# One hymba decoder block: the order of the gate tiles, the evacuation of the v rows, the PSUM banks of two helpers and five lead times of the planner

## The chip, the core and the metric

The kernel runs on one core of one Trainium2 chip. The metric is the device time of one execution in microseconds (us). TensorE (PE) does the matrix products into PSUM, VectorE (DVE) and ScalarE (ACT) read PSUM and work in SBUF, GpSimd (POOL) works in SBUF alone, and SyncE (SP) issues nearly all DMAs. Each engine takes its instructions strictly in its own order and waits on semaphores of the others.

## What is computed

One decoder layer for 1024 tokens and a model width of 1024. Two branches take their inputs from one projection of the normed input; the gates d and z (`z_d`, `z_s`), the three convolved inputs q, k, v and the state-space input u are each 512 wide.

```python
a = rms_norm(h, norm_mix_g)
proj = a @ w_in
u_s, z_s, q, k, v, z_d, b_raw, a_raw = jnp.split(proj, [...], axis=-1)
y_s = s5_branch(u_s, ...) * silu(z_s)          # diagonal state space, gelu, glu
# DeltaNet: q, k, v = silu(causal_conv(q, k, v)); q, k l2-normalised
# beta = sigmoid(b_raw); g = -exp(A_log) * softplus(a_raw + dt_bias)
# chunked gated delta rule over 128 rows, rms_norm, * silu(z_d)
mix = concat([y_s, y_d]) @ w_out
h = h + mix
h = h + sigmoid(h @ w_gate) * rms_norm(p @ w_ple_proj)
return rms_norm(h, final_norm_g)
```

## The kernel before

**Matrix products.** A weight tile of 128 columns is split into a high and a low part (`wh` by ScalarE, `wl` by VectorE), and every product is three matmuls over each of 8 slices of the contraction (`mm3`). An input tile (`inproj`, L615 to 630) makes two halves of 512 tokens; a half is 24 matmuls of 512 columns into one bank, here called for instance q0.0 and q0.1. ScalarE evacuates each half: two activations for q, k and v (`raw` and `cv`), one Silu for the gates d and z (`z`), one copy for u (`ut`). VectorE then does three shifted multiply-adds per convolved tile (`cv<-raw`, L700, recorded under the helper L103).

**PSUM.** The eight banks are in pools: `mm` has two and is taken by turns by `MM` and `MMs` (all halves, the sums of squares `ssp` of q and k, the b tail `pab`, and, before, the v transposes `vtp` and the products k k' `gps`). `MX` has three (the prefix products `pT`). `MS` is one, `MZ` two (S5's `hp`, `kps`, `inj`, `yps`, later the chunks).

**The order.** TensorE's order is written out by a planner (L1326 ff.). It keeps a clock that advances with an estimate of TensorE's work (`pec`), a list of chains, and a list of fillers. A chain yields either a name that must be done or a lead time from the table `LAT` (L474); until its clock time has come, fillers are placed. Other engines' instructions are placed by the framework by readiness. The chains are:

- `a_chain`: 64 steps n for the softplus input a. A step is three matmuls with the triangle (`tg`) and four with the diagonal (`dg`) into `pT`; ScalarE, one VectorE subtraction, ScalarE again, and four VectorE scans (L756) work it off. Steps are planned 5.2 us apart. Then `g_math` (L767) does softplus with small VectorE operations and gives `gg`; TensorE transposes it (`gtp`), a row stage, five transposes (`pe`), `decay`, `subst` (31 steps of a substitution on VectorE), `blocks`, `double` (`q32`, `d32`, `q64`, `d64`) and the eight chunks follow, each chunk in steps A, B and C into the banks `bk`.
- `s5_chain`: S5's parameters on VectorE, then four batches (`hp`, `kps`, a DMA round trip, `inj`, scans, `yps`).
- `attn_chain`: q k' (`kq`) after the loads of q.

Fillers stand in the string `FILL`: input tiles, S5's inputs u, the b columns, k k', GLU (`pg`), the output projections (`po`), the gate (`pq`). A tile of q, k or v may only start when the tail of the tile two before is done. The tails are the sums `ssp` (30.3 us of the clock after the tile), for v the four transposes per half (23.2 us), and for b the product `pab` with `sel` (11.4 us).

Of the kernel before, what the change touches and what calls it, by code (L numbers as in the profile page):

```python
# [16 lines left out]
P = 128  # L17
# [8 lines left out]
def hymba_block_kernel(ctx: ExitStack, tc: tile.TileContext, A: dict, out: bass.AP, dbg=None):  # L26
# [67 lines left out]
    def tt(e, o, a, b, op):  # L94
        return e.tensor_tensor(out=o, in0=a, in1=b, op=op)  # L95
# [277 lines left out]
    def s5_params():  # L373
# [98 lines left out]
    kpv = kp.rearrange("h (b j q) t -> b q j h t", j=4, q=2)  # L472

    LAT = dict(  # L474
        prep=20.0, ev=3.3, kps=5.0, scan=22.0, tab=6.0, g1=23.0, g2=4.0, dec=14.8, sub=25.0, blk=0.3,
        q32=6.9, d32=8.0, q64=2.0, d64=0.8, kq=4.3, A=1.4, B=4.8, C=1.4, otp=10.3, vtp=23.2, ssq=30.3,
        bs8=11.4, gl=15.1, par=13.8, xp=1.2, sse=1.5, ql=14.0,
    )
    s5t = {}

# [286 lines left out]
    def g_math():  # L767
        se = FT[0][:, 0:128].rearrange("p (a b c) -> p a b c", a=4, b=8)
        tt(V, se, se2[:, :, :, :, 0], se2[:, :, :, :, 1], SUB)
        tt(V, se[:, 0], se[:, 0], se[:, 1], ADD)  # L770
        tt(V, se[:, 2], se[:, 2], se[:, 3], ADD)
        tt(V, se[:, 0], se[:, 0], se[:, 2], ADD)
        tt(V, se[:, 0], se[:, 0], hb4[:, 4:8].unsqueeze(1).to_broadcast(SH), ADD)
        ax = flat(se[:, 0])


        gsc = FT[1][:, 0:1024]
        n36 = [0]
# [31 lines left out]
        for c in (0.4985410273075104, 6.578732490539551, 29.91191864013672, 60.949668884277344, 57.11296463012695):  # L810
            stt(V, lp, lp, c, ee, ADD, MUL)
        ts(V, lp, lp, 20.039552688598633, ADD)
        V.tensor_copy(out=lq, in_=ee)
        for c in (15.062909126281738, 83.04756927490234, 221.7624053955078, 309.0987243652344, 216.42788696289062):
            stt(V, lq, lq, c, ee, ADD, MUL)
        ts(V, lq, lq, 60.11865997314453, ADD)
        V.reciprocal(out=lq, in_=lq)
        tt(V, lp, lp, lq, MUL)
        tt(V, l2, ee, ee, MUL)
        tt(V, lq, ee, l2, MUL)  # L820
        tt(V, lp, lq, lp, MUL)
        stt(V, lp, l2, -0.5, lp, MUL, ADD)
        tt(V, lp, ee, lp, ADD)
        ts(V, lx, ee, 1.0, ADD, 0.5, MUL)
        ts(V, lx, lx, -1.0, ADD)
        tt(V, l2, lx, lx, MUL)
        tt(V, lx3, l2, lx, MUL)
        ts(V, la, lx, 0.07037683576345444, MUL)
        stt(V, la, la, -0.11514610052108765, lx, ADD, MUL)
        stt(V, la, la, 0.11676998436450958, lx3, ADD, MUL)  # L830
        ts(V, lb, lx, -0.12420140951871872, MUL)
        stt(V, lb, lb, 0.14249323308467865, lx, ADD, MUL)
        stt(V, lb, lb, -0.16668057441711426, la, ADD, ADD)
        tt(V, lb, lb, lx3, MUL)
        ts(V, lc, lx, 0.2000071406364441, MUL)
        stt(V, lc, lc, -0.24999994039535522, lx, ADD, MUL)
        stt(V, lc, lc, 0.3333333134651184, lb, ADD, ADD)
        tt(V, lc, lc, lx3, MUL)
        ts(V, lc, lc, -0.00021219444170128554, ADD)
        stt(V, l2, l2, -0.5, lx, MUL, ADD)  # L840
        tt(V, lc, l2, lc, ADD)
        ts(V, lc, lc, 0.693359375, ADD)
        ts(V, la, ee, 0.4142135679721832, ALU.is_lt)
        ts(V, lb, la, -1.0, MUL, 1.0, ADD)
        tt(V, lp, lp, la, MUL)
        tt(V, lc, lc, lb, MUL)
# [12 lines left out]
        tr(p[0:32, 0:P], flat(gg_), ident)
        V.tensor_copy(out=gt, in_=p[0:32, 0:P])  # L860
# [12 lines left out]
        ts(V, c2r[:, lo_], gc[:, lo_], gla, SUB)
        V.tensor_copy(out=c2r[:, up_], in_=gc[:, up_])
        V.tensor_copy(out=egr[:, lo_], in_=gc[:, lo_])
        ts(V, egr[:, up_], gc[:, up_], gla, ADD)
        ts(V, err_[:, lo_], c2r[:, lo_], -1.0, MUL, glb, ADD)
        ts(V, err_[:, up_], gc[:, up_], -1.0, MUL, glb, ADD)
        gls = C("gls", [32, 1])
        tt(V, gls, gla, glb, ADD)  # L880
        V.tensor_copy(out=egl_, in_=gls.to_broadcast([32, P]))
        yield LAT["g2"]
        pe5 = MX("pe5", [P, 5, 32])
        for x, r in enumerate((egr, err_, egl_, gc, c2r)):
# [68 lines left out]
    def gram(n):  # L953
        c, i = n // 2, n % 2
        if i == 0:
            zt[c] = T(f"zt{c}", F32, [P, 2, 4, P])
        p = MMs("gps", [P, 4, P])
        for h in range(4):
            mm(p[:, h, :], ksl(kk_, n, h), ksl(kk_, n, h))
        tt(V, zt[c][:, i], p, dd[:, 4 * n:4 * n + 4].unsqueeze(2).to_broadcast([P, 4, P]), MUL)  # L960
        yield 0
        done.add(f"g{n}")

    def v_tile(h):
# [594 lines left out]
```

## Time and profile before

| what | value |
|---|---|
| median of 3 runs | 910.13 us (903.36 to 910.64) |
| the profiled execution, its own time | 910.48 us |
| its span from first to last instruction | 908.7 us |
| PE busy | 795.3 us, 88% |
| DVE busy | 696.9 us, 77% |
| ACT busy | 491.6 us, 54% |
| POOL busy | 256.6 us, 28% |
| mean granted clock of PE | 0.927 |

A busy PE counts the modelled length of its matmuls, at whatever clock was granted; the column PEclk of the stage view tells the clock. The idle time in a row of instructions is that of its engine just before it, and the arrow names who ended it.

### The profile page before, as it was taken

Reading aid. Unit: us, or ns where it says so; the run is one execution under the profiler, and the core shown is the slowest. Engines: PE = TensorE matmul, PEld = TensorE weight load, DVE = VectorE, ACT = ScalarE, POOL = GpSimd, SP = SyncE. Lnnn points to the kernel's source line nnn. Section 1 sums busy time; section 2 is a strip of 40 time slices with the busy share of each in tenths; the row PEclk is TensorE's granted clock in tenths of the full one; section 3 lists DMA queues with packets and bytes.
Section 4 is the critical chain, followed back from the end, with each engine's and each line's share of the span. In section 5 each row is a group of like instructions: output and inputs, shape, how many; then the busy total and the mean of one; then the engine's idle time right before and its main releaser. Section 6 shows DMA issues by size and latency. Waiting matters only on the chain. (4 is left out here: it accounts for less than half of the span.)

```text
span 908.7 us, 12241 instructions
## 1 busy us (share of the span) xinstructions
PE 795.3 (88%) x4338; PEld 647.1 (71%) x4338; DVE 696.9 (77%) x1464; ACT 491.6 (54%) x922; POOL 256.6 (28%) x245
## 2 busy tenths in 40 slices
PE   4689977978995989799798996979899979899996
PEld 3578666856884867688677775868688858678885
DVE  5967968887886599869567989794977695528886
ACT  6678475686676777684768335144432243013343
POOL 0011844541424134503000011035432185302222
PEclk9799979986996997899999998979999998899998
DMA  9331103222031123032300243137562053202211
GB/s 334 128 115 30 64 11 89 83 57 67 9 93 46 53 70 90 27 117 98 90 4 24 70 138 118 67 99 184 151 220 96 33 162 128 70 1 93 75 41 70
DMA packets 67581, 79.93 MB, mean 88 GB/s; under 512 B 23456, under 2 KB 49344, under 8 KB 67520
## 3 DMA queue, kind: packets, MB, share of 16 engines
q1 hardware_dynamic: 67376, 78.89, 27.2%
q8 instruction: 34, 0.56, 0.3%
q10 hardware_dynamic: 144, 0.26, 0.1%
q14 instruction: 27, 0.22, 0.1%
HBM read 57.39 MB, written 21.74 MB: 87 GB/s over the span
## 5 line engine op out<-in xcount | busy, mean ns | idle before, releaser
L115 PE MATMUL pj<-ah,wh 128*128 128x512 f32 x384 | 158.6, 413 | 5.1 <-DVE ssq L914 4.1
L115 PE MATMUL pj<-al,wh 128*128 128x512 f32 x384 | 155.2, 404 | 0.0
L115 PE MATMUL pj<-ah,wl 128*128 128x512 f32 x384 | 155.1, 404 | 0.0
L106 ACT ACTIVATE F<-F,gridc 128x512 f32<-128x512 f32 x128 | 114.9, 987 | 0.0
L756 DVE TENSOR_TENSOR_SCAN F<-F,vst 128x192 f32<-128x192 f32 x128 | 86.9, 740 | 12.6 <-ACT F L106 12.4
L115 PEld LDWEIGHTS pj<-ah,wh 128*128 128x128 f32 x384 | 74.9, 195 | 22.6 <-DVE ssq L914 4.5
L115 PEld LDWEIGHTS pj<-ah,wl 128*128 128x128 f32 x384 | 74.6, 194 | 17.9
L95 DVE TENSOR_TENSOR pT<-F 128x512 f32<-128x512 f32 x64 | 50.2, 784 | 47.9 <-ACT F L106 42.5
L115 PEld LDWEIGHTS pj<-al,wh 128*128 128x128 f32 x384 | 74.9, 195 | 16.2
L756 DVE TENSOR_TENSOR_SCAN F<-F 128x192 f32<-128x192 f32 x128 | 75.6, 647 | 11.2 <-ACT F L106 11.1
L115 PE MATMUL pT<-tg,ah 128*128 128x512 f32 x128 | 56.6, 442 | 12.0 <-ACT F L106 9.8
L115 PE MATMUL pq<-wgl,hth 128*128 128x512 f32 (+1 forms) x200 | 67.0, 387 | 0.0
L106 ACT ACTIVATE F<-pT 128x512 f32<-128x512 f32 x64 | 55.5, 869 | 1.1 <-PE pT L115 1.1
L736 POOL COPY F<-gridc 128x4 f32<-128x4 f32 x32 | 13.4, 420 | 149.9 <-DVE pT L95 92.1
L95 DVE TENSOR_TENSOR h<-h,po 128x512 f32<-128x512 f32 x32 | 21.8, 685 | 37.3 <-PE po L115 37.0
L106 ACT ACTIVATE F<-pT,tbl 128x128 f32<-128x128 f32 x128 | 36.4, 373 | 20.7 <-PE pT L115 20.4
L95 POOL TENSOR_TENSOR e<-e,pleg 128x1024 f32<-128x1024 f32 x8 | 19.4, 2430 | 96.2 <-ACT jq L106 86.7
L103 DVE SCALAR_TENSOR_TENSOR cv<-raw,pk,cv 128x1023 f32<-128x1023 f32 (+2 forms) x36 | 46.5, 1291 | 0.1
L115 PE MATMUL pT<-dg,ah 128*128 128x512 f32 x128 | 43.3, 422 | 2.0 <-DVE pT L95 2.0
L736 POOL COPY F<-tbl 128x4 f32<-128x4 f32 x32 | 15.9, 496 | 98.2 <-DVE pT L95 98.2
L115 PE MATMUL pT<-dg,al 128*128 128x512 f32 x128 | 42.8, 418 | 0.0
L115 PEld LDWEIGHTS pq<-wgl,hth 128*128 128x128 f32 x200 | 37.1, 188 | 7.4
(330 smaller groups left out, 1976.6 us busy)
## 6 DMA issues: line engine op xcount, KB each, us to landing
wr<-in_win SPq DMA_DIRECT2D x24, 512.0 KB, 3.2
x<-in_x SPq DMA_DIRECT2D x8, 512.0 KB, 9.8
wr<-in_wout SPq DMA_DIRECT2D x8, 512.0 KB, 3.3
h<-in_x SPq DMA_DIRECT2D x8, 512.0 KB, 7.1
wr<-in_wgate SPq DMA_DIRECT2D x8, 512.0 KB, 4.8
e<-ed SPq DMA_DIRECT2D x8, 512.0 KB, 3.2
out<-h SPq DMA_DIRECT2D x7, 512.0 KB, 2.6
ed<-e SPq DMA_DIRECT2D x6, 512.0 KB, 8.2
```

The source lines that it names most:

```text
L95: return e.tensor_tensor(out=o, in0=a, in1=b, op=op)
L103: return e.scalar_tensor_tensor(out=o, in0=a, scalar=s, in1=b, op0=op0, op1=op1)
L106: return S.activation(out=o, in_=i, func=f, **k)
L115: return PE.matmul(o, lhsT=l, rhs=r, start=a, stop=z, **k)
L736: G.tensor_copy(out=tb[:, :, 0:1], in_=first)
L756: V.tensor_tensor_scan(out=d0, data0=d0, data1=d1, initial=vst[:, i, h:h + 1] if hf else 0.0, op0=ADD, op1=ADD)
```

## The change

Six edits. **Fillers:** the four d gates stand between the tiles of q and k (`q0 k0 d0 k1 q1 d1 k2 q2 d2 k3 q3 d3`); before, d0 stood after q1, d1 and d2 after q3, and d3 after v3. **v rows:** the evacuation of the v transposes, times the norm of k, is done by ScalarE, one activation per 128 columns, instead of VectorE with one multiplication per 256. **Banks:** the v transposes and k k' take `MS` and `MZ` by turns instead of `mm`. **Softplus:** the three polynomial chains are written in turns (`turns`), with three more scratch tiles and the same operations. **Lead times:** g1 23 to 15, d32 8 to 11, A 1.4 to 2.2, bs8 11.4 to 18, par 13.8 to 18.

```diff
-        prep=20.0, ev=3.3, kps=5.0, scan=22.0, tab=6.0, g1=23.0, g2=4.0, dec=14.8, sub=25.0, blk=0.3,
-        q32=6.9, d32=8.0, q64=2.0, d64=0.8, kq=4.3, A=1.4, B=4.8, C=1.4, otp=10.3, vtp=23.2, ssq=30.3,
-        bs8=11.4, gl=15.1, par=13.8, xp=1.2, sse=1.5, ql=14.0,
+        prep=20.0, ev=3.3, kps=5.0, scan=22.0, tab=6.0, g1=15.0, g2=4.0, dec=14.8, sub=25.0, blk=0.3,
+        q32=6.9, d32=11.0, q64=2.0, d64=0.8, kq=4.3, A=2.2, B=4.8, C=1.4, otp=10.3, vtp=23.2, ssq=30.3,
+        bs8=18.0, gl=15.1, par=18.0, xp=1.2, sse=1.5, ql=14.0,
...
-        lp, lq, l2, lx, lx3, la, lb, lc = (V36()[:, 0:32] for _ in range(8))
-        ts(V, lp, ee, 4.527000055531971e-05, MUL)
...
+        lp, lq, l2, lx, lx3, la, lb, lc, l3, lm, ln = (V36()[:, 0:32] for _ in range(11))
+        def turns(*rows):
+            for i in range(max(map(len, rows))):
+                for r in rows:
+                    if i < len(r):
+                        r[i][0](V, *r[i][1:])
...
+        turns(num, den, large)
...
+        turns(small_, lbs, lcs)
...
-        p = MMs("gps", [P, 4, P])
+        p = (MS, MZ)[i]("gps", [P, 4, P])
...
-                p = MMs("vtp", [P, 2, 2, P])
+                p = (MS, MZ)[n]("vtp", [P, 2, 2, P])
...
-                    tt(V, vr[c][:, :, h, :], p[:, i], sq3[:, 2 * c:2 * c + 2, h:h + 1].to_broadcast([P, 2, P]), MUL)
+                    for j in range(2):
+                        act(vr[c][:, j, h, :], p[:, i, j], AF.Copy, scale=sq3[:, 2 * c + j, h:h + 1])
...
-    FILL = 'u01 b u23 q0 k0 k1 q1 d0 k2 q2 k3 q3 d1 d2 s g v0 v1 v2 v3 d3 z0 z1 z2 z3 l o w x'
+    FILL = 'u01 b u23 q0 k0 d0 k1 q1 d1 k2 q2 d2 k3 q3 d3 s g v0 v1 v2 v3 z0 z1 z2 z3 l o w x'
```

What this does to the engines' orders is shown at three places. The first is PE after the tile k0: `pj_1610` before and `pj_1590` now are its second half k0.1, `pT` the steps of a_chain, `hp` the start of S5's second batch, and `pj_1670` is the half d0.0. Before:

```order
L115 MATMUL pj_1610<-ah7_146,wl_1537 128x512
L115 MATMUL pT_1663<-tg2_1458,ah2_141 128x512
L115 MATMUL pT_1663<-tg2_1458,al2_149 128x512
L115 MATMUL pT_1663<-tg2_1458,ah2_141 128x512
L115 MATMUL pT_1582<-dg2_1457,ah2_141 128x512 x2
L115 MATMUL pT_1582<-dg2_1457,al2_149 128x512 x2
L115 MATMUL pT_1683<-tg2_1458,ah2_141 128x512
L115 MATMUL pT_1683<-tg2_1458,al2_149 128x512
L115 MATMUL pT_1683<-tg2_1458,ah2_141 128x512
L115 MATMUL pT_1623<-dg2_1457,ah2_141 128x512 x2
L115 MATMUL pT_1623<-dg2_1457,al2_149 128x512 x2
L119 MATMUL hp_1703<-cm_90,s5x1_863 128x128 x4
```

And now:

```order
L115 MATMUL pj_1590<-ah7_146,wl_1489 128x512
L115 MATMUL pj_1670<-ah0_139,wh_1665 128x512
L115 MATMUL pj_1670<-al0_147,wh_1665 128x512
L115 MATMUL pj_1670<-ah0_139,wl_1664 128x512
L115 MATMUL pj_1670<-ah1_140,wh_1665 128x512
L115 MATMUL pj_1670<-al1_148,wh_1665 128x512
L115 MATMUL pj_1670<-ah1_140,wl_1664 128x512
L115 MATMUL pT_1677<-tg2_1458,ah2_141 128x512
L115 MATMUL pT_1677<-tg2_1458,al2_149 128x512
L115 MATMUL pT_1677<-tg2_1458,ah2_141 128x512
L115 MATMUL pT_1562<-dg2_1457,ah2_141 128x512 x2
L115 MATMUL pT_1562<-dg2_1457,al2_149 128x512 x2
```

The steps of a_chain that followed each other with no half between them now have d0 between them. In the same way d2 stands where, after q2, four steps followed each other before. At the end of the tiles it is the other way round: behind d3.1 five steps, one `ssp`, `yps` and then the products k k' follow each other with no half between; before, it was two steps, `yps` and k k' behind d2.1.

The second place is PE at the b tail. `pj_1023` is the half u3.0 in both, `pj_1110` is u2.1, and `pab` is the b tail. Before:

```order
L115 MATMUL pj_1023<-ah3_142,wh_971 128x512
L115 MATMUL pj_1023<-al3_150,wh_971 128x512
L115 MATMUL pj_1023<-ah3_142,wl_970 128x512
L115 MATMUL pab_1075<-sel_427,s8_885 128x4 x8
L115 MATMUL pj_1023<-ah4_143,wh_971 128x512
L115 MATMUL pj_1023<-al4_151,wh_971 128x512
```

And now:

```order
L115 MATMUL pj_1023<-ah7_146,wl_970 128x512
L115 MATMUL pj_1110<-ah0_139,wh_964 128x512
L115 MATMUL pj_1110<-al0_147,wh_964 128x512
L115 MATMUL pj_1110<-ah0_139,wl_963 128x512
L115 MATMUL pj_1110<-ah1_140,wh_964 128x512
L115 MATMUL pj_1110<-al1_148,wh_964 128x512
L115 MATMUL pj_1110<-ah1_140,wl_963 128x512
L115 MATMUL pj_1110<-ah2_141,wh_964 128x512
L115 MATMUL pj_1110<-al2_149,wh_964 128x512
L115 MATMUL pj_1110<-ah2_141,wl_963 128x512
L115 MATMUL pab_1120<-sel_427,s8_870 128x4 x8
```

Before, `pab` stood in the middle of u3.0 and took the bank that u2.0 had left; now it stands nine matmuls into u2.1, which itself takes u2.0's bank, so that `pab` takes u3.0's.

The third place is DVE at the end of softplus. `gg` is its result, `cv<-raw` the convolutions of the v tiles, `wl` the split of a weight tile, `F_406` the scratch of softplus, and the copy of `gtp` follows the transpose on PE. Before:

```order
L100 TENSOR_SCALAR F_406<-F_406 128x32
L95 TENSOR_TENSOR wl<-wr,wh 128x1024
L99 TENSOR_SCALAR F_406<-F_406 128x32
L103 SCALAR_TENSOR_TENSOR cv<-raw,pk,cv 128x1023
L95 TENSOR_TENSOR F_406<-F_406 128x32
L103 SCALAR_TENSOR_TENSOR cv<-raw,pk,cv 128x1022
L99 TENSOR_SCALAR F_406<-F_406 128x32
L103 SCALAR_TENSOR_TENSOR cv<-raw,pk,cv 128x1021
L95 TENSOR_TENSOR F_406<-F_406 128x32 x2
L103 SCALAR_TENSOR_TENSOR F_406<-F_405,F_406 128x32
L95 TENSOR_TENSOR gg<-F_406 128x32
L860 COPY F_407<-gtp 32x128
```

And now:

```order
L95 TENSOR_TENSOR F_406<-F_406 128x32
L824 RECIPROCAL F_406<-F_406 128x32
L103 SCALAR_TENSOR_TENSOR F_406<-F_406 128x32
L95 TENSOR_TENSOR F_406<-F_406 128x32 x3
L99 TENSOR_SCALAR F_406<-F_406 128x32
L95 TENSOR_TENSOR F_406<-F_406 128x32 x2
L103 SCALAR_TENSOR_TENSOR F_406<-F_406 128x32
L99 TENSOR_SCALAR F_406<-F_406 128x32
L95 TENSOR_TENSOR F_406<-F_406 128x32 x4
L103 SCALAR_TENSOR_TENSOR F_406<-F_405,F_406 128x32
L95 TENSOR_TENSOR gg<-F_406 128x32
L865 COPY F_407<-gtp 32x128
```

The convolution of v3 and one weight split have left the way to `gg`; they now stand behind it, in the decay stage. On PE `gtp` now stands 21 matmuls into v3.0, which is 69 matmuls of 512 columns after the last step of a_chain; before, it stood six matmuls into d3.1, 126 after it.

More of the change, by code (lines that the diff above doesn't have):

```diff
@@ L807, in g_math @@
         ee, nea = fq[:, 0:32], fq[:, 32:36]
-        lp, lq, l2, lx, lx3, la, lb, lc = (V36()[:, 0:32] for _ in range(8))
-        ts(V, lp, ee, 4.527000055531971e-05, MUL)
[L810 to L829, printed above, removed]
@@ L840, in g_math @@
-        stt(V, l2, l2, -0.5, lx, MUL, ADD)
-        tt(V, lc, l2, lc, ADD)
+        lp, lq, l2, lx, lx3, la, lb, lc, l3, lm, ln = (V36()[:, 0:32] for _ in range(11))
[4 more added lines that the diff above has]
+                        r[i][0](V, *r[i][1:])
+        num = [(ts, lp, ee, 4.527000055531971e-05, MUL)] + [
+            (stt, lp, lp, c, ee, ADD, MUL)
+            for c in (0.4985410273075104, 6.578732490539551, 29.91191864013672, 60.949668884277344, 57.11296463012695)
+        ] + [(ts, lp, lp, 20.039552688598633, ADD)]
@@ new lines, in g_math @@
+        den = [(lambda e, o, i: e.tensor_copy(out=o, in_=i), lq, ee)] + [
+            (stt, lq, lq, c, ee, ADD, MUL)
+            for c in (15.062909126281738, 83.04756927490234, 221.7624053955078, 309.0987243652344, 216.42788696289062)
+        ] + [(ts, lq, lq, 60.11865997314453, ADD), (lambda e, o, i: e.reciprocal(out=o, in_=i), lq, lq)]
+        large = [
+            (ts, lx, ee, 1.0, ADD, 0.5, MUL), (ts, lx, lx, -1.0, ADD), (tt, l3, lx, lx, MUL), (tt, lx3, l3, lx, MUL),
+            (ts, la, lx, 0.07037683576345444, MUL),
+            (stt, la, la, -0.11514610052108765, lx, ADD, MUL),
+            (stt, la, la, 0.11676998436450958, lx3, ADD, MUL),
+        ]
@@ new lines, in g_math @@
+        turns(num, den, large)
+        small_ = [
+            (tt, lp, lp, lq, MUL), (tt, l2, ee, ee, MUL), (tt, lq, ee, l2, MUL), (tt, lp, lq, lp, MUL),
+            (stt, lp, l2, -0.5, lp, MUL, ADD), (tt, lp, ee, lp, ADD),
+        ]
+        lbs = [
+            (ts, lb, lx, -0.12420140951871872, MUL), (stt, lb, lb, 0.14249323308467865, lx, ADD, MUL),
+            (stt, lb, lb, -0.16668057441711426, la, ADD, ADD), (tt, lb, lb, lx3, MUL),
+        ]
+        lcs = [
+            (ts, lc, lx, 0.2000071406364441, MUL), (stt, lc, lc, -0.24999994039535522, lx, ADD, MUL),
+            (ts, lm, ee, 0.4142135679721832, ALU.is_lt), (ts, ln, lm, -1.0, MUL, 1.0, ADD),
+        ]
@@ L842, in g_math @@
+        turns(small_, lbs, lcs)
+        turns([
+            (stt, lc, lc, 0.3333333134651184, lb, ADD, ADD), (tt, lc, lc, lx3, MUL),
+            (ts, lc, lc, -0.00021219444170128554, ADD),
+        ], [(stt, l3, l3, -0.5, lx, MUL, ADD), (tt, lp, lp, lm, MUL)])
+        tt(V, lc, l3, lc, ADD)
         ts(V, lc, lc, 0.693359375, ADD)
[L843 to L846, printed above, removed]
+        tt(V, lc, lc, ln, MUL)
```

10 lines of the change are left out of this document (removed).

## The prediction

> **What bounds the kernel now.** I read the page's busy times first, then the stages, then PE's waits.
>
> ```profile
> PE 795.3 (88%) x4338; PEld 647.1 (71%) x4338; DVE 696.9 (77%) x1464; ACT 491.6 (54%) x922; POOL 256.6 (28%) x245
> ```
>
> PE leads with 88%, so a change pays by removing idle PE time, or slow clock. Where that lies is told by the stages, cut at the ends of halves:
>
> ```profile
> core 0: us, PE busy (x) PEld busy (x) DVE busy (x) ACT busy (x) POOL busy (x), PEclk, DMA share, GB/s
> 193.66:221.09 27.43, 17.68 (x85) 13.16 (x85) 24.97 (x37) 21.99 (x40) 11.94 (x15) 0.72 0.11 38
> 221.09:334.15 113.06, 103.51 (x554) 84.92 (x555) 84.21 (x121) 76.64 (x141) 35.44 (x38) 0.92 0.21 59
> 334.15:356.68 22.53, 18.22 (x93) 15.19 (x92) 22.46 (x29) 16.86 (x34) 11.36 (x12) 0.70 0.13 41
> 356.68:441.04 84.36, 76.65 (x391) 61.47 (x390) 67.70 (x106) 59.34 (x108) 23.20 (x26) 0.94 0.28 85
> ...
> 497.00:604.10 107.10, 93.29 (x539) 75.30 (x539) 93.11 (x238) 40.30 (x61) 12.09 (x8) 0.94 0.27 94
> 604.10:908.70 304.60, 277.90 (x1652) 230.26 (x1652) 214.71 (x577) 104.06 (x249) 99.56 (x53) 0.94 0.32 103
> ```
>
> The two short stages at 193.66 and 334.15 hold four steps of a_chain each and no half. There DVE is busy 24.97 of 27.43 and 22.46 of 22.53 us: DVE bounds them, while PE idles and its clock falls to 0.72 and 0.70. In the long ones between (113.06 and 84.36 us) PE is busy over 90%. From the last step of a_chain (497) to the first `d` product (604) DVE is busy 93.11 of 107.10 us: a chain through softplus, decay and substitution sets that stage, and PE fills it with v, d3 and z. The last 304.6 us are PE's (277.90 busy). PE's waits by name:
>
> ```profile
> PE ssp L115 <- ACT z L106: 12.4, 2, 9.6
> ...
> PE bk L115 <- ACT rt L106: 7.1, 7, 1.8
> ...
> PE vtp L119 <- ACT z L106: 6.4, 1, 6.4
> PE pab L115 <- ACT ut L106: 6.4, 1, 6.4
> ...
> PE d L115 <- DVE qs L1103: 3.7, 1, 3.7
> ```
>
> Apart from those at the start, which no edit touches, most are waits for one of the two `mm` banks, which ScalarE empties late. Such a wait costs more than itself, because the clock falls during it:
>
> ```profile
> 273.81:283.36 9.55, 0.00 (x1) 0.00 (x1) 7.24 (x14) 9.46 (x16) 2.41 (x4) 0.70 0.45 109
> 283.36:291.30 7.94, 7.94 (x27) 6.97 (x28) 4.96 (x7) 0.49 (x2) 4.80 (x7) 0.50 0.00 0
> ```
>
> After the wait of 9.55 us PE works 7.94 us at 0.50, so 4.0 us more are lost.
>
> **The sum, part by part.** It is made against the profiled execution: 908.7 us span, 910.48 us of its own, 0.35 above the median of 910.13.
>
> *The d gates.* A d tile is 48 matmuls. At full clock that many take 11.06 us:
>
> ```profile
> 805.87 11.06 PE pq L115 x48
> ```
>
> d0 and d2 move into the two stages that DVE bounds. PE's 17.68 us there at 0.72 are 12.7 us of full clock; with 11.06 it is 23.8, under 27.43. In the other it is 12.8 + 11.06 = 23.8 against 22.53. Each brings one weight split on DVE, 1.22 us by the row below: +1.2 and +1.3 us. Out of the stage at 356.68, which has eight halves in 84.36 us, 10.5 us each, two go: -21.1. But the 48 matmuls had 2.7 steps of a_chain between them (18 matmuls a step), and these now stand bare behind d3.1, at the pace of the bare stages, (27.43 + 22.53) / 8 = 6.2 us: +16.7. The slow clock that reaches from the first bare stage into PE's stage behind it (0.84 over 16.60 us) costs 2.7 us now; the new bare stage behind d3.1 will hand the same to v0, so these cancel:
>
> ```profile
> 221.09:237.69 16.60, 16.60 (x93) 13.62 (x94) 9.81 (x16) 10.22 (x21) 3.55 (x4) 0.84 0.17 40
> ```
>
> Together -1.9. Bounds: -12 if the bare steps run in the shadow of k k', +10 if d0's and d2's 11.06 us each lengthen their stages by half of that instead.
>
> *The b tail.* ScalarE and PE there:
>
> ```profile
> 113.81 0.21 ACT L106 ACTIVATE vst<-F 128x4 f32<-128x4 f32 x1 [7.42 <-DVE F L756]
> ...
> 118.24 1.01 ACT L106 ACTIVATE ut<-pj 128x512 f32<-128x512 f32 x1
> 119.07 1.10 ACT L106 ACTIVATE F<-pT,tbl 128x128 f32<-128x128 f32 x4
> 120.04 0.87 ACT L106 ACTIVATE F<-pT 128x512 f32<-128x512 f32 x1
> 120.72 1.78 ACT L106 ACTIVATE F<-F,gridc 128x512 f32<-128x512 f32 x2
> 122.34 1.07 ACT L106 ACTIVATE s5h<-hp 128x512 f32<-128x512 f32 x2
> ```
>
> ```profile
> 119.31 3.57 PE L115 MATMUL pab<-sel,s 8*128 8x4 f32 x16 [6.36 <-ACT ut L106]
> ```
>
> `pab` waits 6.36 us for u2.0's bank, since ScalarE was held 7.42 us by DVE's scans. More clock lets u3.0 finish first, but the next half, u2.1, needs that same bank and so also starts at 119.3. Nine matmuls on (2.1 us, 121.4) `pab` needs u3.0's bank, and between u2.0's and u3.0's evacuations ScalarE has two steps of a_chain (2 x 3.75 us) and `s5h` (1.07): about 128.6. I expect the wait to change its bank, some 7 us long, and S5's round trip behind it to start later by as much as the halves are ahead: 0. Bounds: -10 (6.36 and the slow clock behind it, priced as above) and +4. The lead of S5's parameters goes with it.
>
> *From the last step to the products `d`.* DVE's work in softplus, from its start to `gg`:
>
> ```profile
> L103 DVE SCALAR_TENSOR_TENSOR cv<-raw,pk,cv 128x1021 f32<-128x1021 f32 x3 | 3.8, 1274 | 0.0
> ...
> L95 DVE TENSOR_TENSOR F<-F 128x32 f32<-128x32 f32 x16 | 2.8, 187 | 0.3
> ...
> L103 DVE SCALAR_TENSOR_TENSOR F<-F 128x32 f32<-128x32 f32 x18 | 2.4, 183 | 0.1
> L95 DVE TENSOR_TENSOR wl<-wr,wh 128x1024 fp32r<-128x1024 f32 x2 | 2.4, 1220 | 1.2 <-ACT wh L106 1.2
> ...
> L95 DVE TENSOR_TENSOR vr<-vtp,sqk 128x256 f32<-128x256 f32 x4 | 1.6, 420 | 1.6 <-PE vtp L119 1.6
> ```
>
> By the order three multiply-adds of v3 (3 x 1.27 = 3.8), one split (1.2), four rows `vr` (1.7) leave this stretch, and with them the waits of 1.6 and 1.2: 9.5. The turns spare the latency between dependent small operations. The trace does not show it apart; the two rows of small ones (2.8 + 2.4 = 5.2 us) bound it between 0 and half of that, 2.6; I take 1. Behind `gg` the three multiply-adds come back (+3.8), eight `vr` go:
>
> ```profile
> L95 DVE TENSOR_TENSOR vr<-vtp,sqk 128x256 f32<-128x256 f32 x8 | 2.9, 405 | 0.4 <-PE vtp L119 0.4
> ```
>
> That is -9.5 - 1 + 3.8 - 2.9 = -9.6; some of the waits will return elsewhere, so I take -8.5 (bounds -12 and -3). PE cannot gain more here: DVE's chain sets the stage, and PE has one tile less to fill it with. So PE will stand at `gtp`. It gets there 69 matmuls (15.9 us) and 16 transposes after the last step, while the chain needs what it needed:
>
> ```profile
> 533.07 0.28 DVE L860 COPY F<-gtp 32x128 f32<-32x128 f32 x1 [0.38 <-PE gtp L119]
> ```
>
> 533.07 - 497.00 = 36.1, less about 9.5: 26 us. This idle time of 8 us, and about as much before `q32`, costs nothing by itself, nor do d32's extra matmuls save anything: they shift PE's wait for the same DVE copies.
>
> *v rows on ScalarE and the banks.* 32 activations, nearest row 373 ns each at the same shape, are 11.9 us on ScalarE, which is busy 40.30 of 107.10 us in that stage; DVE loses 16 x 0.41 us, counted above:
>
> ```profile
> L106 ACT ACTIVATE F<-pT,tbl 128x128 f32<-128x128 f32 x128 | 36.4, 373 | 20.7 <-PE pT L115 20.4
> ```
>
> The waits of `vtp` (6.4) vanish into the same stage and are not counted again. k k' keeps two banks, and its waits stay. The Trainium skill, page "ScalarE: Activation LUTs", section "Rules for kernel authors", speaks against this edit: multiplications belong on VectorE. By its figures (186 ns, 93 for a pointer operand, 0.833 per element) one activation is an estimated 386 ns and all 32 are 12.3 us. The row agrees on the price; what the rule leaves out is which engine the stage waits for.
>
> *A, from 1.4 to 2.2.* Three more `po` matmuls stand between a chunk's steps A and B. The 7.1 us of `bk` waits are mostly in the last chunks, after the fillers have run out, and chunk 6 loses the matmuls between B and C: 0, bounds -2 and +2.
>
> Sum: -1.9 + 0 - 8.5 + 0 = -10.4, so 910.48 - 10.4 = **900 us**.
>
> **Rivals.**
>
> *The waits go as meant.* `pab` finds its bank free (-10 by the bound) and the bare steps at the end hide behind k k' (some -3 more): 887 us. For it: u3.0's evacuation need not be that late if ScalarE's steps come earlier. Against: DVE holds ScalarE there whatever PE does. Chance 0.2.
>
> *The tiles are not absorbed.* PE pays 11.06 us for the tile that now lies ahead of the last step, at the full price, for which the bare steps give back little: the d gates are +5, the chain keeps -8.5, 907 us, no change that can be told (1% is about what a measurement of this kernel can tell). For it: ScalarE's 21.99 of 27.43 us and DVE's 91% leave little room. Chance 0.25.
>
> *ScalarE becomes late.* The 11.9 us of v rows stand ahead of the exponentials and Silus in its queue and delay the chain by what DVE gained, 6.6 us: 907 us. The skill's rule would have it so; a ScalarE busy 38% of the stage speaks against. Chance 0.05.
>
> *Slower: the sums behind the halves.* Four `ssp` now stand six matmuls (1.4 us) behind a half whose bank they need. Before, one such place cost the 9.55 us and 4.0 behind it. With d0 and d2 in the bare stages ScalarE and DVE get no pause to catch up. If each of three more costs half of that, 6.8 us: 900 + 20 = 920 us. It decides from 6.5 us each on. Against: the other such wait was 2.8 us (12.4 - 9.6). Chance 0.13.
>
> **How the numbers follow.** The forecast case, 893 to 907 with 900 as its middle, has chance 0.37; over half of it is under 901, the bound of 1%. Faster: 0.2 + 0.23 + 0.02 from the others' lower tails, 0.45, and I give 0.47 because a wait removed also spares the slow clock; slower: 0.13 and a little of the upper tails, 0.15; same 0.38. The range leaves out a tenth at each end: down to 884 (the first rival and 3 us), up to 915 (between the second rival and the last).
>
> **What would show it.** Right: no idle PE over 3 us near 190 to 215 and 335 to 350; a bare stretch of PE behind d3.1 with DVE near its full time; `pab` still waiting for `ut`, now behind u2.1; an idle PE of 5 to 10 us at `gtp` released by `gg`; softplus on DVE shorter by 8 to 10 us; table loads and ScalarE's share hardly changed. Wrong: `gtp` not waited for, or several waits of `ssp` over 5 us, or a time outside 884 to 915.

## The result, and the profile after

The changed kernel takes 932.08 us (median of 4 runs, 930.58 to 933.94) beside 910.37 us before (median of 4). The ratio on record is 1.0246, 95% interval 1.0206 to 1.0286; the two medians themselves give 1.0238. The forecast was 900 us. The profiled execution took 930.58 us, its span is 928.9 us, at a mean granted clock of 0.915 (before 0.927).

The page of the changed kernel first, its line of busy times:

```profile
PE 799.8 (86%) x4338; PEld 654.6 (70%) x4338; DVE 686.1 (74%) x1448; ACT 499.3 (54%) x953; POOL 261.8 (28%) x245
```

PE has the same 4338 instructions and is busy 4.5 us more (795.3 before), which is slower clock. The rest of the 20.2 us by which the span grew is idle PE. Where it idles is told by PE's waits in the changed kernel (in total, times, longest):

```profile
PE ssp L115 <- ACT z L106: 16.6, 3, 12.1
PE ssp L115 <- ACT cv L106: 11.8, 3, 7.6
...
PE q L115 <- DVE q L1086: 7.0, 1, 7.0
PE pab L115 <- ACT vst L106: 6.7, 1, 6.7
PE gtp L119 <- DVE gg L95: 6.4, 1, 6.4
...
PE pg L115 <- ACT gh L106: 5.0, 1, 5.0
```

The sums `ssp` wait 28.4 us in six places (12.9 in three before), `pg` 10.8 (5.0, and 3.7 for `sg` and 2.1 for `gl`; 1.6 before), and `q` and `gtp` 13.4 together, where before neither waited. Gone are the 6.4 us of `vtp` and 3.7 of `d`. One of the six waits of `ssp`, on PE and then on ScalarE, which PE waits for:

```profile
297.07 3.15 PE L115 MATMUL ssp<-cm,raw 128*128 128x1 f32 x14 [12.06 <-ACT z L106]
```

```profile
289.14 0.21 ACT L106 ACTIVATE se<-F 128x8 f32<-128x8 f32 x1 [1.87 <-DVE F L756]
289.37 1.28 ACT L106 ACT_TABLE_LOAD   x1
290.66 1.09 ACT L106 ACTIVATE s5x<-yps 128x512 f32<-128x512 f32 x2
...
295.13 1.28 ACT L106 ACT_TABLE_LOAD   x1
296.42 0.60 ACT L106 ACTIVATE z<-pj 128x512 f32<-128x512 f32 x1
```

PE has run ahead: the half d1.0 ended at 283.62, its evacuation `z` starts 12.8 us later. In front of it ScalarE works off S5's `yps`, a step of a_chain (the rows left out, 291.63 to 295.12) and two table loads. Six matmuls into d1.1, `ssp` needs that bank. What the wait leaves behind it shows in the windows of the wait and of the same time after it:

```profile
284.70:297.10 12.40, 0.34 (x3) 0.03 (x1) 9.04 (x14) 10.44 (x18) 3.64 (x4) 0.69 0.46 111
297.10:309.30 12.20, 12.20 (x42) 10.39 (x43) 6.59 (x10) 3.49 (x7) 5.82 (x7) 0.61 0.00 0
```

12.20 us of work at 0.61 would be 7.4 at full clock: 4.8 us more are lost.

The b tail in the changed kernel, PE and the activation that empties its bank:

```profile
128.56 0.58 PE L115 MATMUL pab<-sel,s 8*128 8x4 f32 x2 [6.68 <-ACT vst L106]
```

```profile
127.44 1.06 ACT L106 ACTIVATE ut<-pj 128x512 f32<-128x512 f32 x1
```

`ut` of u3.0 ends at 128.50, and `pab` starts at 128.56; the forecast said 128.6. From softplus on, by windows (the bare steps behind d3.1, the rest of the steps, softplus to `gg`, `gg` to the first `d`, and the rest):

```profile
445.16:485.43 40.27, 30.17 (x179) 25.42 (x177) 31.97 (x50) 26.33 (x53) 10.86 (x11) 0.87 0.15 40
485.43:522.48 37.05, 37.05 (x166) 30.20 (x165) 25.53 (x42) 29.66 (x61) 0.54 (x1) 1.00 0.08 29
522.48:540.28 17.80, 11.47 (x54) 9.12 (x52) 17.01 (x81) 7.58 (x16) 0.00 (x0) 0.95 0.20 61
540.28:613.97 73.69, 66.67 (x410) 54.72 (x410) 64.44 (x130) 29.47 (x56) 9.73 (x7) 0.87 0.29 101
613.97:928.90 314.93, 279.79 (x1653) 233.95 (x1652) 207.90 (x573) 105.33 (x251) 100.74 (x54) 0.92 0.31 99
```

Softplus to `gg` fell from 27.44 us (505.25 to 532.69) to 17.80: 9.6 less, the forecast's sum of 9.5 and 1 within an us. But it starts 17.2 us later, since a_chain ends later; `gg` to `d` grew by 2.3, and the last stage from 304.6 to 314.9. So the loss is 17.2 - 9.6 + 2.3 + 10.3 = 20.2 us.

### The profile page after: what moved, and what is told of

Its sections match the earlier page's. It is cut to its first block, busy times and chain, and to the rows that moved or that the text cites. A ratio compares the mean times of both kernels' runs of the same rounds, so it can differ in the third digit from the quotient of the medians.

```text
span 928.9 us, 12257 instructions
## 1 busy us (share of the span) xinstructions
PE 799.8 (86%) x4338; PEld 654.6 (70%) x4338; DVE 686.1 (74%) x1448; ACT 499.3 (54%) x953; POOL 261.8 (28%) x245
## 5 line engine op out<-in xcount | busy, mean ns | idle before, releaser
L756 DVE TENSOR_TENSOR_SCAN F<-F,vst 128x192 f32<-128x192 f32 x128 | 87.1, 741 | 11.5 <-ACT F L106 11.3
L756 DVE TENSOR_TENSOR_SCAN F<-F 128x192 f32<-128x192 f32 x128 | 71.7, 617 | 13.0 <-ACT F L106 13.0
L736 POOL COPY F<-tbl 128x4 f32<-128x4 f32 x32 | 18.3, 572 | 108.5 <-DVE pT L95 108.5
L95 DVE TENSOR_TENSOR h<-h,po 128x512 f32<-128x512 f32 x32 | 21.9, 685 | 33.3 <-PE po L115 33.2
L115 PE MATMUL ssp<-cm,raw 128*128 128x1 f32 x128 | 21.1, 295 | 28.4 <-ACT z L106 16.6
L115 PEld LDWEIGHTS ssp<-cm,raw 128*128 128x128 f32 x128 | 20.8, 253 | 31.2 <-ACT z L106 17.9
```

The lines of the kernel that those rows point to most:

```text
L115: return PE.matmul(o, lhsT=l, rhs=r, start=a, stop=z, **k)
L736: G.tensor_copy(out=tb[:, :, 0:1], in_=first)
L756: V.tensor_tensor_scan(out=d0, data0=d0, data1=d1, initial=vst[:, i, h:h + 1] if hf else 0.0, op0=ADD, op1=ADD)
```

## The experiments

"Good kernel" below is the kernel before with the turns in softplus, the v rows and the banks (e3). Each ratio is to the kernel before on the same chip; the us are (ratio - 1) times that kernel's median.

| kernel | median us | ratio, 95% interval | us |
|---|---|---|---|
| the change | 932.08 | 1.0246, 1.0206 to 1.0286 | +22.4 |
| e1 gates alone | 919.76 | 1.0098, 1.0072 to 1.0124 | +8.9 |
| e2 all but the gates | 915.28 | 1.0059, 1.0044 to 1.0074 | +5.4 |
| e3 softplus, v rows, banks | 900.15 | 0.9899, 0.9882 to 0.9915 | -9.2 |
| e4 all but the leads | 912.03 | 1.0025, 1.0007 to 1.0043 | +2.3 |
| e5 e3 with bs8, par | 912.03 | 1.0038, 1.0014 to 1.0062 | +3.5 |
| e6 e3 with g1, d32 | 906.84 | 0.9971, 0.9940 to 1.0002 | -2.6 |
| e7 e3 with A | 902.52 | 0.9929, 0.9896 to 0.9962 | -6.5 |
| e8 change, z stored elsewhere | 930.52 | 1.0230, 1.0185 to 1.0275 | +20.9 |
| e9 change, `ssp` in MS | 917.47 | 1.0103, 1.0074 to 1.0132 | +9.4 |
| e10 e3, `ssp` in MS | 898.41 | 0.9899, 0.9860 to 0.9937 | -9.2 |
| e11 e10, `pab` in MS too | 904.95 | 0.9960, 0.9942 to 0.9979 | -3.6 |
| e12 change, bs8 and par old | 909.63 | 1.0005, 0.9979 to 1.0030 | +0.5 |
| e13 change, z3 ahead of q32 | 921.34 | 1.0123, 1.0071 to 1.0175 | +11.2 |
| e14 turns alone | 909.77 | 1.0009, 0.9973 to 1.0045 | +0.8 |
| e15 v rows and banks alone | 900.18 | 0.9897, 0.9852 to 0.9942 | -9.4 |
| e16 e12, `ssp` in MS | 898.29 | 0.9886, 0.9835 to 0.9938 | -10.4 |
| e17 banks alone | 906.66 | 0.9975, 0.9950 to 1.0000 | -2.3 |
| e18 v rows alone | 911.75 | 1.0029, 1.0004 to 1.0054 | +2.6 |

### Which edit: e1 to e4

e1 is the kernel before with this alone:

```diff
-    FILL = 'u01 b u23 q0 k0 k1 q1 d0 k2 q2 k3 q3 d1 d2 s g v0 v1 v2 v3 d3 z0 z1 z2 z3 l o w x'
+    FILL = 'u01 b u23 q0 k0 d0 k1 q1 d1 k2 q2 d2 k3 q3 d3 s g v0 v1 v2 v3 z0 z1 z2 z3 l o w x'
```

> The kernel before with the new order of the gates alone; the other five edits are left out. Theory: in the changed kernel the steps of a_chain end 17 us later (last scan 505.3 to 522.6), because the two bare stretches did not take in a tile (11 us) and the sums ssp wait 28 us instead of 13. Softplus keeps its length here, so the first product d should come about 17 us later too; some 18 matmuls of pg now stand ahead of d and give back about 4: 923 us. Rival (the lead times did it, the gates are worth what I forecast): 908 to 910 us, with the last scan within 3 us of 505.

It cost 8.9 us. The last scan came 5.6 us later (510.9), not 17. In the same run `ssp` waits 18.1 us instead of 12.9, so how much of the 5.6 is work that the bare stretches did not take in, and how much is these waits, is not told apart. Then PE, with one tile less to fill the stage, stood at q32:

```profile
604.96 1.27 PE L115 MATMUL q<-q,zt 32*32 32x32 f32 x39 [13.03 <-DVE q L1080]
```

And the substitution before q32 took 34.9 us instead of 30.3, with the same 62 operations. With d3 ahead of the last step, the z tiles end sooner, so GLU's weights and inputs are split on POOL while VectorE substitutes. What that does shows best in e4, VectorE and POOL in the same stretch:

```profile
590.56 0.36 DVE L95 TENSOR_TENSOR xt<-q,q 128x192 f32<-128x192 f32 x1
590.95 2.91 DVE L95 TENSOR_TENSOR q<-q,xt 128x192 f32<-128x192 f32 x1
593.89 2.87 DVE L95 TENSOR_TENSOR xt<-q,q 128x175 f32<-128x175 f32 x1
```

```profile
590.68 5.88 POOL L95 TENSOR_TENSOR gl<-gr,gh 128x1024 fp32r<-128x1024 f32 x2 [3.90 <-ACT gh L106]
```

An operation of 0.36 us takes 2.9 when one of POOL's, of 2.9 each, runs. Over the substitution's 62 operations the durations add up to 21.2 us in the kernel before, where none of POOL's products stands beside them, to 23.4 in e3 with one, 27.1 in e1 with three and 32.7 in e4 with six: about 2 us for each. The changed kernel hardly has this loss: its substitution takes 28.4 us, with one of POOL's products beside it.

e2 takes that edit out of the changed kernel, e3 takes out the leads too, e4 the leads alone:

```diff
-        ... g1=15.0 ... d32=11.0 ... A=2.2 ... bs8=18.0 ... par=18.0 ...
+        ... g1=23.0 ... d32=8.0 ... A=1.4 ... bs8=11.4 ... par=13.8 ...
```

> The changed kernel with the old order of the gates; all other edits are in. Theory (gates cost 17, softplus and v rows give 9.6, lead times cost some 6 behind d): 910 - 9.6 + 6 = 906 us, last scan at 505 to 509, gg some 9 us sooner than before. Rival (the lead times for the b tail and S5 make a_chain late): last scan stays at 515 or later and the time is 920 us or more.

> The kernel before with the turns in softplus, the v rows on ScalarE and the banks for v and k k'; order of the gates and lead times are the old ones. Theory: DVE's way to gg is 9.6 us shorter as in the changed kernel, PE had 13 us of waits in that stage to lose, so first d some 8 us sooner: 902 us. Rival (PE fills the stage and sets it, as its 93.3 of 107 us may mean): 907 us or more, with the waits of vtp gone and a new wait of PE in their place.

> The changed kernel with the five old lead times. Theory: gates +17 on the last scan, softplus -9.6, and the waits of pg for gh (5.0, 2.1, 3.7 us) gone, since z3.1 stands ahead of q32 again and the load of gr behind z3 on SP comes sooner: 932 - 10 = 922 us at most, nearer 915. Rival (the lead times cost nothing, the late pg is the gates' doing): 930 us, with pg waiting as long as in the changed kernel.

e3 came as expected: 9.2 us gained, close to the forecast's 8.5, with PE's order unchanged. e4 says the gates cost 11.5 on top of that: its last scan is 9.3 us later than e3's, the substitution 8.9 longer, and PE stands 20.0 us at q32. e2 missed: the leads cost 14.6 us on e3, not 6, though the last scan came at 507.8, in the range of the theory. They lose behind the scans: the first `pg` stands at 628.6 instead of 603.0 in e3. In e2, 57 matmuls of z stand behind q32 and none of `pg` ahead of the first `bk`; in e3 it is none of z and 45 of `pg`. Taken out of the changed kernel, the gates are worth 17.0 us (e2) and the leads 20.1 (e4), more than each costs without the other. So the largest item is one that the prediction had at nothing.

### Which lead: e5, e6, e7, e12

> Softplus in turns, v rows and banks (the kernel of 900.15 us), and of the five lead times only bs8 (18) and par (18). Theory (S5 late): first inj 8 us later and the k k' products some 5 us later, as in the kernel with all leads; the time is 903 to 906 us, a third to a half of the 15 us that all five leads cost together. Rival (these two leads are neutral, as I forecast): 900 us, within 2.

> The kernel of 900.15 us with g1 = 15 and d32 = 11 alone. Theory (PE's idle time at gtp and q32 is not free, since the matmuls that should have filled it are left for the stage behind d, where PE has none idle, and z3 is late, so that pg waits for gh): gtp waits some 6 us and q32 about as much, first d 4 to 6 us later, the time 907 us. Rival (idle time there costs nothing, as the prediction has it): 900 us, within 2.

> The kernel of 900.15 us with A = 2.2 alone. Theory (no gain, small loss, since a chunk that stands without a filler comes at the end: twenty bk matmuls in a row now): 901 us, from 899 to 903. Rival (A carries the loss of the chunks, 13 us between the first and the last bk): 908 us or more.

> The changed kernel with bs8 and par set back (11.4 and 13.8); gates, g1, d32 and A stay new. Theory (these two leads are the dearest of the five, 12.6 us on the kernel of 900 us, through the places of ssp against the halves): 917 to 920 us, with the waits of ssp back under 19 us. Rival (with the gates between q and k the sums collide anyway): 928 us or more.

On e3, bs8 and par cost 12.6 us (0.0139), far more than the 3 to 6 expected; g1 and d32 6.5, as expected; A 2.7, its interval overlapping e3's. In the changed kernel, setting bs8 and par back won 21.9 us (0.0241): e12 stands level with the kernel before, better than expected. e5's waits show what these two leads do:

```profile
PE pj L115 <- DVE ssk L919: 14.7, 3, 6.5
...
PE ssp L115 <- ACT cv L106: 9.3, 2, 5.8
```

In e3, halves wait 0.3 us for a bank that `ssp` of k holds (`ssk`); in e5 14.7. S5's first `inj` moved from 145.1 to 154.0, every later piece of S5 in PE's order with it, and so the places of the sums against the halves. In e12, to be read beside the change:

```profile
PE ssp L115 <- ACT z L106: 11.9, 2, 9.5
...
PE ssp L115 <- ACT cv L106: 4.7, 1, 4.7
```

`ssp` waits 16.6 us instead of 28.4; in the same view `pg` waits 1.8 instead of 10.8 and `gtp` 2.5 instead of 6.4. The order tells why: in e12 `gtp` stands 21 matmuls further on, and all of z3 stands ahead of q32. With the gates, then, g1, d32 and A cost nothing that can be told: e12, which has them, is level with e4, which does not (-1.8 us), and in both all of z stands ahead of q32 and 63 matmuls of `pg` ahead of the first `bk`. On e3, e5 and e6 leave just nine there instead of 45.

### The sums' bank: e9, e10, e11, e16

e9 changes one word and leaves PE's order as it is, so that only the bank differs:

```diff
-        p = MMs("ssp", [P, 8])
+        p = MS("ssp", [P, 8])
```

> The changed kernel with one edit: the sums ssp take the bank MS instead of a turn in mm; PE's order stays the same to the last matmul. Theory (the sums behind a half wait for its bank, 28.4 us in the changed kernel, and this, with the slow clock behind it, is most of what the gates lost): the waits of ssp fall under 8 us, half of what goes comes back as waits of the halves, and the time is 915 to 920 us. Rival (ScalarE and DVE are full there, so PE waits at the next half instead): idle PE before the halves and pT grows by what ssp loses, 930 us.

13 us of 22 went with it, as the theory said. But what came back does not stand at the halves: `pg` still waits 12.3 us. What `ssp` and S5, which now share MS, still cost each other is in e9's waits:

```profile
PE ssp L115 <- ACT s5x L106: 7.9, 2, 6.3
...
PE hp L119 <- DVE ssq L919: 6.6, 1, 6.6
```

> The kernel of 900.15 us (softplus in turns, v rows, banks; old gates and leads) with the sums ssp in MS. Theory: of the waits of ssp (12.9 us) and of halves for a bank that ssp holds (4.1) most go, and the slow clock behind the wait of 9.6 with them (4 us): 888 to 892 us. Rival (moved on): 899 us.

> As the run before, and the b tail pab in MS too. Theory: pab's wait of 6.4 us goes, but S5's chain behind it is bound by its own round trip, so half of it comes back at inj: 3 us less than the run before, 885 to 889 us. Rival (ScalarE is held by the scans there, and the next half waits): the same time as the run before.

> The changed kernel with bs8 and par set back, and the sums ssp in MS. Theory (the sums wait 16.6 us there, half of it comes back): 900 us, level with the kernel that has softplus and the v rows alone. Rival (as there, MS is S5's too, and what ssp saves kps loses): 908 us.

On the good kernel the same word won nothing, as the rival had it. e10's waits:

```profile
PE pT L115 <- ACT F L106: 12.0, 5, 4.8
PE kps L115 <- ACT s5h L106: 10.9, 4, 4.4
```

There `ssp` had cost 12.9 us; `kps` now waits 10.9 instead of 2.7 and `pT` 2.2 more. I read this as ScalarE's lateness, which shows at whatever next needs ScalarE. e11 missed the other way: `pab` in MS waits 10.0 us for S5's `hp` instead of 6.4 in `mm`, and the kernel lost 5.6 against e10. In e16 `ssp` waits 1.4 us and `kps` 10.1 (4.6 in e12), yet 10.9 us of e12's time go. It is level with e3 within the intervals. So the bank is worth 13, 11 or nothing by the order around it.

### Why `pg` is late: e8, e13

The rows of the changed kernel, ScalarE, then POOL, then PE:

```profile
613.82 1.06 ACT L106 ACTIVATE wgh<-wgr 128x1024 fp32r<-128x1024 f32 x1 [7.53 <-issue]
614.78 0.58 ACT L106 ACTIVATE z<-pj 128x512 f32<-128x512 f32 x1
622.88 3.76 ACT L106 ACTIVATE gh<-gr 128x1024 fp32r<-128x1024 f32 x2 [7.52 <-DMA gr<-yd]
```

```profile
614.96 2.35 POOL L95 TENSOR_TENSOR wgl<-wgr,wgh 128x1024 fp32r<-128x1024 f32 x1 [17.51 <-ACT wgh L106]
```

```profile
624.86 0.80 PE L115 MATMUL pg<-gh,wgh 128*128 128x512 f32 x1 [5.03 <-ACT gh L106]
```

My first theory was SP's queue: the loads of `gr` stand there behind the store of z3.

```diff
-        SP.dma_start(out=zsd[m] if kind else zdd[:, m, :], in_=z)
+        (S if kind else SP).dma_start(out=zsd[m] if kind else zdd[:, m, :], in_=z)
```

> The changed kernel with one edit: the z tiles are stored through ScalarE's DMA queue instead of SP's, so that the loads of gr no longer stand on SP behind the store of z3. Theory (pg waits 10.8 us because gr is loaded late, and gr stands behind z3): gh comes at about 606 instead of 623, the waits of pg shrink to some 2 us, and the time falls by 6 to 9 us to about 924 us. Rival (gr's buffers, or the chunks behind, hold the end whatever SP does): 932 us, within 2.

It fell: `gr` was issued at 617.85 instead of 617.33, and the time is the same within the intervals. In both, that is just when POOL's `wgl` ends (614.96 + 2.35 = 617.31), so I read it as `gr` waiting for the buffer that `wgr` leaves. Ahead of `wgl` stands `wgh`, and that starts at 613.82, 0.3 us after z3.1's last matmul starts. That half now ends at 614.04, since PE stood 7.0 us at q32 with nine of its matmuls behind. e13 moves these nine ahead by one lead:

```diff
-        prep=20.0, ev=3.3, kps=5.0, scan=22.0, tab=6.0, g1=15.0, g2=4.0, dec=14.8, sub=25.0, blk=0.3,
+        prep=20.0, ev=3.3, kps=5.0, scan=22.0, tab=6.0, g1=15.0, g2=4.0, dec=14.8, sub=27.5, blk=0.3,
```

> The changed kernel with the planner's lead for the substitution 27.5 instead of 25: the last nine matmuls of z3.1 then stand ahead of q32 (nine more of pg too), in idle time of PE; nothing ahead of that moves. Theory (wgh takes the weight buffer that z3.1 still reads, so gh and pg are late): wgh at about 601 instead of 614, gh by 610 instead of 623, the waits of pg fall from 10.8 to under 4 us, and the time is 922 to 926 us. Rival (what is not waited for at pg is waited for at bk): 931 us.

The time fell by 11.2 us (0.0123), a little more than expected. ScalarE in e13:

```profile
608.08 3.40 ACT L106 ACTIVATE zt<-z 32x256 f32<-32x256 f32 x8 [2.46 <-DVE z L1085]
611.50 1.06 ACT L106 ACTIVATE wgh<-wgr 128x1024 fp32r<-128x1024 f32 x1
612.63 1.99 ACT L106 ACTIVATE gh<-gr 128x1024 fp32r<-128x1024 f32 x1
```

`gh` comes 10.3 us sooner and the waits of `pg` are 0.9 us. `wgh` is later than the 601 that I expected, because the copies `zt` now stand ahead of it. So the nine matmuls of z3.1 behind q32 are shown as the cause, together with nine of `pg` that the same lead places ahead of the first `bk` (45 instead of 36). The link is not shown: in e13 the first load of `gr` is issued at 608.34, ahead of that `wgl` (612.63) and 2.7 us behind the store of z3, and only the second `gr` right behind the end of `wgl` (615.08). More than one buffer may hand the lateness on.

### Softplus or v rows: e14, e15, e17, e18

e14 has the function `turns` alone, e15 the other two edits of that stage; e17 and e18 split e15:

```diff
-        p = MMs("gps", [P, 4, P])
+        p = (MS, MZ)[i]("gps", [P, 4, P])
...
-                p = MMs("vtp", [P, 2, 2, P])
+                p = (MS, MZ)[n]("vtp", [P, 2, 2, P])
```

```diff
-                    tt(V, vr[c][:, :, h, :], p[:, i], sq3[:, 2 * c:2 * c + 2, h:h + 1].to_broadcast([P, 2, P]), MUL)
+                    for j in range(2):
+                        act(vr[c][:, j, h, :], p[:, i, j], AF.Copy, scale=sq3[:, 2 * c + j, h:h + 1])
```

> The kernel before with the turns in softplus alone. Theory (the order of the writing decides where the framework puts v3's convolution and the splits, so most of the 9.6 us belong to the turns): gg 6 to 8 us sooner, but vtp still waits 6.4 us: 904 us. Rival (the v rows made the room, by their four rows and the waits before them): gg within 3 us of before, 908 us.

> The kernel before with the v rows on ScalarE and the banks alone. Theory: vtp's waits go, DVE loses 3.3 us of rows on its way to gg; gg 3 us sooner: 906 us. Rival (the v rows carry it): gg 7 us sooner or more, 902 us.

> The kernel before with the banks of the v transposes and of k k' alone; VectorE still evacuates the v rows. Theory (two legs meet at gtp: VectorE's way to gg and TensorE's tiles; the vtp waits of 9.7 us are TensorE's leg, and the rows behind them are VectorE's): TensorE reaches gtp sooner, but gg stays within 3 us of before and TensorE waits for it: 905 us, about half of the gain. Rival (the banks are all): 900 us.

> The kernel before with the v rows on ScalarE alone; the v transposes and k k' keep their turns in mm. Theory: vtp still waits for a half's bank (6 us or more), gg comes 3 to 6 us sooner, and TensorE is late at gtp: 907 to 909 us. Rival (the rows are all): 900 us.

The turns alone win nothing, the other two together all of it, and neither of these two alone more than 2.3. e14 and e15 missed their theories, by 6 us each way; e17 and e18, built with the two legs in mind, came within 3 us. The reason is at `gtp`, where two legs meet: DVE's way to `gg` and PE's tiles. In the kernel before they end together; PE there:

```profile
532.46 0.40 PE L115 MATMUL pj<-ah,wl 128*128 128x512 f32 x1
532.75 0.28 PE L119 MATMUL gtp<-cm,gg 128*32 128x128 f32 x1
```

In e14 and in e18 DVE's leg, from the last scan to the end of `gg`, is shorter (20.3 us in both, 27.4 before) and PE's is not. `gg`, then the copy of `gtp`, in e14:

```profile
527.13 0.19 DVE L95 TENSOR_TENSOR gg<-F 128x32 f32<-128x32 f32 x1
...
534.73 0.28 DVE L865 COPY F<-gtp 32x128 f32<-32x128 f32 x1 [1.17 <-PE gtp L119]
```

and in e18:

```profile
523.72 0.19 DVE L95 TENSOR_TENSOR gg<-F 128x32 f32<-128x32 f32 x1
...
536.06 0.28 DVE L860 COPY F<-gtp 32x128 f32<-32x128 f32 x1 [1.18 <-PE gtp L119]
```

PE reaches `gtp` at 534.4 and 535.7, since `vtp` still waits 9.6 and 9.9 us. In e17 PE's leg is shorter and DVE's is not, and PE waits for `gg`:

```profile
530.26 0.28 PE L119 MATMUL gtp<-cm,gg 128*32 128x128 f32 x1 [2.22 <-DVE gg L95]
```

e15 shortens both, and they end together again; DVE, then PE:

```profile
526.50 0.19 DVE L95 TENSOR_TENSOR gg<-F 128x32 f32<-128x32 f32 x1
```

```profile
526.75 0.28 PE L119 MATMUL gtp<-cm,gg 128*32 128x128 f32 x1 [0.21 <-DVE gg L95]
```

## Why the prediction was wrong

**The steps that failed.** Three terms of the prediction carry the miss; two are here, the third is the d gates below. "This idle time of 8 us, and about as much before `q32`, costs nothing by itself" priced the shifts of the leads g1 and d32 and of the tile taken from behind the steps at nothing. The size of the idle time was right (6.4 and 7.0 us). But from `d` on PE is the bound, as the prediction's first part says, and its matmuls are fixed in number: what it has not done when `d` comes, it does afterwards. e6 shows it: there `d` comes 1.5 us and the first `bk` 6.2 us sooner than in e3, and the end of the span 8.6 us later, for 36 matmuls of `pg` that e3 places ahead of the first `bk` now stand behind it. In the changed kernel e13 won 11.2 us by moving nine matmuls of z3.1 ahead of q32. The price is not a fixed one: with the gates and the old bs8 and par the same leads cost nothing (e12 beside e4), and there no matmul of z or `pg` is left behind. The second is "I expect the wait to change its bank [...] 0" with bounds of -10 and +4 for bs8 and par. The wait did change its bank, to 0.1 us as worked out, and that part of the round trip came out at 8 us, as far as the halves were ahead. The bounds were too narrow, since they looked at `pab` alone; and in no run did `pab` find its bank free, as the bound of -10 and the first rival have it. S5's batches come later in the planned order ever after, and with them the sums (six waits instead of three), `gtp` 21 matmuls sooner, and z3.1 behind q32. The measured price is 21.9 us in this kernel, 12.6 on e3.

**The d gates.** Forecast -1.9 (bounds -12 and +10), measured +8.9 alone, +11.5 on e3 and +17.0 in the changed kernel. PE no longer idles in the former bare stretches but for 3.7 us at 195.6, and a bare stretch stands behind d3.1, as forecast; its DVE is busy 31.97 of 40.27 us, so it is not DVE alone that bounds it. So the term was mis-sized. Missing from the sum were more waits of `ssp` (in e1 5.2 us more) and, in e1 and e4, the longer substitution; in the changed kernel it is not longer, and there the last scan comes 17.2 us later, of which e9 gives 12.0 back (510.5 instead of 522.6) by the bank of `ssp` alone. How much of a tile the stretches take in, no run shows by itself.

**From the last step to `d`.** Forecast -8.5, measured -9.2 (e3). The size was right, but partly by luck, for the reasons are half wrong. "PE cannot gain more here: DVE's chain sets the stage" is refuted by e14 and e18: a DVE leg 7 us shorter wins nothing. "The waits of `vtp` vanish into the same stage and are not counted again" is the same error; they were PE's leg of a tie. The turns are worth 0.8 us the wrong way, within their interval, where 1 was taken. On DVE's own leg the 1 us fits: from e15 to e3 it falls by 4.9 us, of which v3's three multiply-adds are 3.8; it is worth nothing because PE arrives later. The sum also left out that the weight split comes back behind `gg` (1.2 us); taking -8.5 for -9.6 covered that.

**v rows on ScalarE.** The price was right: 379 ns each in the changed kernel, beside 373 of the row and the estimated 386 from the Trainium skill's page "ScalarE: Activation LUTs", section "What ACT_TABLE_LOAD costs".

```profile
L106 ACT ACTIVATE vr<-vtp,sqk 128x128 f32<-128x128 f32 x32 | 8.9, 379 | 1.4 <-PE vtp L119 1.4
```

The same page of the Trainium skill, section "Rules for kernel authors", gives a multiplication to VectorE because it is faster per element (its figure is for bf16). The rows agree with that: 405 to 420 ns for 256 columns on VectorE, 379 for 128 on ScalarE. What the edit is worth is another matter: by itself it cost 2.6 us (e18), in company with the banks it won 7.1 (e17 to e15).

**A.** Forecast 0 within 2, measured +2.7 on e3 with overlapping intervals: not told apart from 0.

**The rivals.** "Slower: the sums behind the halves" is what came, with 15.5 us more of waits where 20 in all were priced, two of them over 5 us (12.1 and 7.6); e9 confirms it with 13.0 us. It got a chance of 0.13. Against it stood that another such wait had been 2.8 us. That was one place; the order shows six, each six or thirteen matmuls behind a half, and nothing in the rows promised that they would be short. That the tiles are not absorbed was half true at most: the gates cost more than its +5, but the tiles' part in that is not told apart from the waits. That ScalarE becomes late through the v rows did not happen: the stretch to `gg` is 9.6 us shorter.

**Not foreseen:** the 9.2 us more of waiting at `pg`. The order showed nine matmuls of z3.1 behind q32; I read them as filler, and not as work that GLU's loads and weights wait for.

What the runs leave open: the effects do not add. The parts measured apart (gates 8.9, turns with v rows -9.2, and on top of e3 12.6, 6.5 and 2.7) sum to 21.5, near the 22.4 measured, but e2 gives 14.6 for all leads together where their parts sum to 21.8, and e4 and e12 give -1.8 for g1, d32 and A with the gates. Part of the reason is in the order: bs8 with par, and g1 with d32, each push z and `pg` behind the same places, so on e3 both lose the same thing, while with the gates and the old bs8 and par nothing of either is pushed behind. The other part, which sum meets which half, no run isolates. Nor does a run have e9's and e13's edits together, so whether their 13.0 and 11.2 us add up is open. Of all kernels, e16 has the lowest median (898.29) and e15, with two edits, the same time within the intervals (900.18).

## What to carry to other kernels

Idle time on the engine that is the bound later is not to be taken as free: its work is fixed, so count the matmuls that the new order leaves behind the wait. Here leaving 36 behind went with 6.5 us lost, and leaving none with no loss. Where two legs meet at one instruction within a fraction of an us, a cut on one leg wins little or nothing (here 2.3 us at most, of 9.4 for both); look at when the producer ended and when the consumer arrived, and cut both. Before a lead time is changed, follow the new order to the end of the program for three things: small products that need the bank of a half just issued, a tile that ends late and holds what something later waits for, and how many matmuls are left behind the last chain.

## What the runs showed of the hardware

VectorE's operations on two SBUF operands were held up by POOL's products of two SBUF operands: the rows of e4 above show two, each stretched to the end of one of POOL's, 0.36 us to 2.91 and 2.87. The Trainium skill, page "SBUF — State Buffer", section "SBUF: two separate sides", states it as an exclusive lock on a port pair that the two engines share, held for a whole instruction, against a POOL operation that reads SBUF; the rows agree. POOL's share of time, 28%, does not tell whose operations it will meet.

The same order of matmuls can run 5 us apart, and the granted clock shows where. e13 and the changed kernel have the same order up to q32, but e13's last scan ended at 527.7 and the other's at 522.6. Between 310 and 360 us PE was busy nearly all the time in both, but the mean clock was 1.00 in the changed kernel and 0.93 in e13, which got 18 matmuls fewer done; later stretches take some back and add some. The changed kernel, then e13:

```profile
310.00:360.00 50.00, 48.83 (x283) 39.41 (x282) 39.37 (x60) 37.06 (x67) 12.31 (x14) 1.00 0.20 67
```

```profile
310.00:360.00 50.00, 48.62 (x265) 39.27 (x263) 36.24 (x56) 34.87 (x64) 12.58 (x14) 0.93 0.18 56
```

So a difference below 5 us needs the medians of several runs, and not one profile each.
